# Stick-breaking weights from differenced values, and a re-ordered opening, in a fused encoder block

## The chip, the cores and the metric

One core of a Trainium2 chip runs the whole kernel as one program. The metric is device time in microseconds (us) of that core; lower is better. Engines are TensorE (PE, its weight loads PEld), VectorE (DVE), ScalarE (ACT), GpSimd (POOL) and SyncE (SP, which only issues transfers). The core has 16 DMA engines, which all queues share.

## The reference, cut to what matters

One layer over 512 tokens and 1024 channels, float32. The opening is an adaLN-modulated RMS norm and the input projection:

```python
mod = c_act @ mod_w[l] + mod_b[l]
sh1, sc1, g1, sh2, sc2, g2 = [m[:, None, :] for m in jnp.split(mod, 6, axis=-1)]
h = rms_norm(x, norm1_g[l]) * (1.0 + sc1) + sh1
proj = h @ w_in[l]
```

The columns of `proj` go to a convolution branch, an HGRN2 recurrence and stick-breaking attention (8 heads of 64), whose core, per block of 128 queries, is

```python
z = jnp.einsum('bhtd,bhsd->bhts', qb, kb).astype(jnp.float32) * scale
mask = s_pos[None, :] < t_pos[:, None]
log_keep = jnp.where(mask, jax.nn.log_sigmoid(-z), 0.0)
between = lax.cumsum(log_keep, axis=3, reverse=True) - log_keep
a = jnp.where(mask, jnp.exp(jax.nn.log_sigmoid(z) + between), 0.0)
outs.append(jnp.einsum('bhts,bhsd->bhtd', a.astype(vb.dtype), vb))
```

The three branches are gated, summed and projected; a squared-ReLU MLP follows.

## The kernel before, in words

The kernel is one Python function that records instructions; a scheduler then fixes the order in each engine's queue. From there on each engine takes its queue strictly in order, and an instruction that waits holds up all behind it. Products are float32 split in a rounded part and a rest (`hilo`, L83 on ACT and L84 on DVE), so each product is three matmuls (`mm3`, L113 to L115).

**Opening.** For each of eight blocks j of 128 input channels it needs a scale and a shift column from `mod_w`. `prep_mod(j)` multiplies eight 128x256 pieces of the loaded tile `ms` by `cact` and adds them up (two on ACT, L236, six on DVE, L238), adds the two partial sums (L241) and sums over the partitions with two matmuls against ones (`tp`, L245). `prep_h(j)` transposes the normed x (`tq`, L254), scales and shifts it into `s` (ACT, L258) and splits it into `ht`. `prep_w(j)` splits the 384 KB slab of `w_in`. `first_mm(j)` then issues 18 matmuls into six accumulators (`mm` and `f`). The loads `ms` (two halves of 512 KB for each j, three buffers) and `slab` stand in SP's queue behind the four tiles of x; the small `vecs` and `conv_w` (31 rows of 2 KB) go on ACT's queue.

**Attention.** `sv_in` copies the value rows out of PSUM (L521). For each pair of heads `sb_split` splits queries and keys (ACT L507 to L510, DVE L508 and L511), and `sb_weights` makes scores `z` (PE, L539 to L541), takes sigmoid(-z) and sigmoid(z) (ACT, L88, tile `bt`), scans the first into running products (DVE, L545) and multiplies the second by it (DVE, L546); `sb_turn` transposes the weights (PE, L557), ACT copies them back (L560), and PE multiplies them with the values (L573). Gate products `g` of `head_gate` and the convolution's taps (`cv`, DVE, L462) are recorded beside it and fill gaps.

The scheduler's order is the order of work; `tc.issue_after(x)` keeps instructions behind instruction x on x's engine.

Of the kernel before, what the change touches and what calls it, by code (L numbers as in the profile page):

```python
# [13 lines left out]
ALU = mybir.AluOpType  # L14
# [24 lines left out]
def tile_hybrid_block(ctx, tc, x, vecs, mod_w, mod_b, w_in, conv_w, w_conv, w_hgrn, w_sb, w_out, w1, w2, out):  # L39
# [42 lines left out]
    def hilo(src, hi, lo):  # L82
        A.activation(hi, src, AF.Copy)  # L83
        V.tensor_tensor(out=lo, in0=src, in1=hi.bitcast(F32), op=ALU.subtract)  # L84

    def after(bi, *args, **kw):
        with tc.issue_after(bi.ins):
# [22 lines left out]
    def mm3(o, lhs, rhs, start, stop):  # L110
        lh, ll = lhs
        rh, rl = rhs
        TE.matmul(o, lhsT=lh, rhs=rh, start=start, stop=False)  # L113
        TE.matmul(o, lhsT=lh, rhs=rl, start=False, stop=False)  # L114
        TE.matmul(o, lhsT=ll, rhs=rh, start=False, stop=stop)  # L115


    vrow = S((NVEC, P), g="c0")
    A.dma_start(vrow, vecs)
    cw_row = S((CW, 512), g="c0")  # L120
    A.dma_start(cw_row, conv_w)
# [40 lines left out]
    eps = C([P, 1], F32)  # L162
    G.memset(eps, EPS)
    scanm = C([P, NT, P], F32)
    G.memset(scanm, 1.0)
    G.memset(scanm[:, :, 0:1], 0.0)
# [6 lines left out]
    cp = ax()  # L173
    for i in range(4):
        TE.transpose(cp[:, i * 32:i * 32 + CW], cw_row[:, i * P:(i + 1) * P], ident[0:CW, 0:CW])
    cwc = C([P, 4, 32], F32)
    V.tensor_copy(cwc[:, :, 0:CW], cp[:, 0:128].rearrange("p (i k) -> p i k", k=32)[:, :, 0:CW])
# [9 lines left out]
    oml = C([P, 4], F32)  # L187
    lb = vcol[:, V_HLB:V_HLB + 4]
    lbe = C([P, 4], F32)
    lbs = C([P, 4], F32)  # L190
    V.tensor_tensor(out=lbe, in0=lb, in1=lb, op=ALU.subtract)
    ph(lbe, lbe, AF.Exp)
    V.reciprocal(out=lbs, in_=lbe)
    V.tensor_tensor(out=lbe, in0=lbe, in1=lbs, op=ALU.mult)
    V.tensor_tensor(out=lbs, in0=lbe, in1=lbe, op=ALU.subtract)
    V.tensor_scalar(out=oml, in0=lbs, scalar1=-1.0, scalar2=1.0, op0=ALU.mult, op1=ALU.add)

    gbh = C([P, 24], F32)
    V.tensor_scalar(out=gbh, in0=vcol[:, V_GB:V_GB + 24], scalar1=0.5, scalar2=None, op0=ALU.mult)
    lnh = C([P, 8], F32)  # L200
    V.tensor_scalar(out=lnh, in0=vcol[:, V_LG:V_LG + 8], scalar1=0.5, scalar2=None, op0=ALU.mult)
# [7 lines left out]
    modc = C([P, 16], F32)  # L209


    facc = [mm() if i < 4 else ps("f") for i in range(6)]
    hT, fw = [], {}


    def rstd_small(dst, ssq, n):
# [5 lines left out]
    def x_norm(t):  # L222
        junk = P4((P, D), g="x0")
        after(first, junk, xt[t], AF.Square, accum_out=stat[:, t:t + 1])
        rstd_small(stat[:, 4 + t:5 + t], stat[:, t:t + 1], D)
        V.tensor_scalar(out=xt[t], in0=xt[t], scalar1=stat[:, 4 + t:5 + t], scalar2=None, op0=ALU.mult)

    def prep_mod(j):
        ms = ms_t.pop(j)
        acc = S((P, 2, 2, P), g="acc")  # L230
        for kk in range(KT):
            a, src, c = acc[:, kk % 2], ms[:, :, kk, :], cact[:, kk:kk + 1]
            if kk < 2 and j == 0:
                V.tensor_scalar(out=a, in0=src, scalar1=c, scalar2=None, op0=ALU.mult)
            elif kk < 2:
# [27 lines left out]

    def prep_w(j):
# [4 lines left out]
    def prep(j):  # L269
        load_ms(j)  # L270
        load_slab(j)
        prep_mod(j)
        prep_h(j)
        prep_w(j)

    def first_mm(j):
        wh, wl = fw.pop(j)
        for i in range(6):
            c = slice(i * P, (i + 1) * P)
            mm3(facc[i], (wh[:, c], wl[:, c]), hT[j], j == 0, j == KT - 1)  # L280


    wu = ps("tq")
    for i in range(8):
        TE.matmul(wu, lhsT=ident, rhs=scanm.rearrange("p a t -> p (a t)"), start=True, stop=True)
    for t in range(NT):
        x_norm(t)
    prep_mod(0)
    prep_h(0)
    prep_w(0)  # L290
# [209 lines left out]
    def sb_split(i):  # L500
# [22 lines left out]

    so2 = [P4(g="so") for _ in range(2)]
# [271 lines left out]
    hnh = C([P, 1], F32)  # L796
    V.tensor_scalar(out=hnh, in0=vcol[:, V_HN:V_HN + 1], scalar1=0.5, scalar2=None, op0=ALU.mult)

    for h in range(4):
        k_in(h)  # L800
# [277 lines left out]
```

## Time and profile before

| | |
|---|---|
| median of 3 runs | 922.27 us (921.96 to 922.89) |
| the profiled execution, its own time | 924.09 us |
| its span, first to last instruction | 922.3 us |
| busy PE | 894.8 us (97%) |
| busy DVE | 599.5 us (65%) |
| busy ACT | 385.8 us (42%) |
| mean granted TensorE clock | 0.996 |

Busy time is the union of an engine's instructions. What counts for the time is where PE has none: 27.5 us of the span. The profiled execution is 1.8 us above the median; its span equals the median to 0.1 us.

### The profile page before, as it was taken

How to read it: one execution, taken by the hardware profiler on the slowest of the kernel's cores; microseconds unless marked ns; L12 is line 12 of the kernel's file. 1: busy time of each engine (PE TensorE's matmuls, PEld its weight loads, DVE VectorE, ACT ScalarE, POOL GpSimd, SP SyncE). 2: the span in 40 equal slices, each digit the busy share in tenths (PEclk: the TensorE clock that was granted, in tenths of full speed). 3: DMA queues.
4: the chain of work that ended last, by engine and by line, in shares of the span. 5: the costliest groups of instructions: out<-in, count | busy, mean ns of one | idle time of the engine just before them, and what ended most of it. 6: DMA issues, size and time to landing. Idle time of an engine off the chain costs nothing.

```text
span 922.3 us, 10624 instructions
## 1 busy us (share of the span) xinstructions
PE 894.8 (97%) x4185; PEld 728.8 (79%) x4185; DVE 599.5 (65%) x886; ACT 385.8 (42%) x596; POOL 28.1 (3%) x35
## 2 busy tenths in 40 slices
PE   4999989999988999999999999999999999999998
PEld 2788878888755588888888888888888888888886
DVE  4882388899999999997965544774423254442422
ACT  4652434475788632223833536453312123431210
POOL 1002000001032000000000000000000000000000
PEclk9999999999999999999999999999999999999999
DMA  9981301131200344793423620552242233142121
GB/s 279 279 268 59 113 12 46 52 132 46 91 1 1 115 159 162 245 329 136 138 86 103 216 70 1 192 196 91 92 137 92 56 113 106 46 137 92 68 69 46
DMA packets 85418, 107.78 MB, mean 117 GB/s; under 512 B 2270, under 2 KB 58705, under 8 KB 85368
## 3 DMA queue, kind: packets, MB, share of 16 engines
q1 hardware_dynamic: 85200, 106.96, 35.5%
q8 instruction: 33, 0.54, 0.3%
q14 instruction: 17, 0.14, 0.1%
q10 hardware_dynamic: 168, 0.14, 0.0%
HBM read 105.00 MB, written 2.10 MB: 116 GB/s over the span
## 4 chain that ended last, share of the span: by engine, by line
PE 88%; DVE 6%; ACT 3%; DMA 2%; issue 1%; SPq 1%; DVEq 0%; ACTq 0%
PE mm L113 14%; PE mm L114 14%; PE mm L115 14%; PE ax L115 9%; PE ax L113 9%; PE ax L114 9%; PE o L115 2%; PE o L114 2%; PE o L113 2%; PE g L113 2%; PE g L114 2%; PE g L115 2%; PE g L654 1%; DVE bt L545 1%; PE o L573 1%; DVE bt L546 1%
## 5 line engine op out<-in xcount | busy, mean ns | idle before, releaser
L84 DVE TENSOR_TENSOR wl<-w,wh 128x1024 fp32r<-128x1024 f32 x134 | 162.8, 1221 | 194.4 <-ACT wh L83 147.4
L83 ACT ACTIVATE wh<-w 128x1024 fp32r<-128x1024 f32 x134 | 139.8, 1054 | 290.8 <-PE ax L115 129.9
L113 PE MATMUL mm<-ht,wh 128*128 128x512 f32 x272 | 106.7, 392 | 0.0
L115 PE MATMUL mm<-ht,wl 128*128 128x512 f32 x272 | 106.6, 392 | 0.0
L114 PE MATMUL mm<-ht,wh 128*128 128x512 f32 x272 | 106.6, 392 | 0.0
L114 PE MATMUL mm<-p,wh 128*128 128x512 f32 (+1 forms) x272 | 102.6, 378 | 0.0
L115 PE MATMUL mm<-p,wl 128*128 128x512 f32 (+1 forms) x272 | 102.4, 377 | 0.0
L113 PE MATMUL mm<-p,wh 128*128 128x512 f32 (+1 forms) x272 | 102.3, 377 | 0.0
L462 DVE SCALAR_TENSOR_TENSOR cv<-cv,cbig 128x511 f32<-128x511 f32 (+29 forms) x120 | 83.5, 733 | 0.0
L113 PEld LDWEIGHTS mm<-ht,wh 128*128 128x128 f32 x272 | 51.1, 188 | 11.2 <-issue 0.8
L114 PEld LDWEIGHTS mm<-ht,wh 128*128 128x128 f32 x272 | 51.1, 188 | 11.0 <-issue 0.6
L115 PEld LDWEIGHTS mm<-ht,wl 128*128 128x128 f32 x272 | 51.1, 188 | 10.4 <-issue 0.2
L114 PEld LDWEIGHTS mm<-p,wh 128*128 128x128 f32 x272 | 51.2, 188 | 9.4
L115 PEld LDWEIGHTS mm<-p,wl 128*128 128x128 f32 x272 | 51.2, 188 | 9.4
L113 PEld LDWEIGHTS mm<-p,wh 128*128 128x128 f32 x272 | 51.0, 188 | 9.3
L113 PE MATMUL ax<-wh,p 128*128 128x512 f32 x128 | 49.8, 389 | 0.0
L114 PE MATMUL ax<-wl,p 128*128 128x512 f32 x128 | 49.8, 389 | 0.0
L115 PE MATMUL ax<-wh,p 128*128 128x512 f32 x128 | 49.8, 389 | 0.0
L113 PE MATMUL ax<-wh,s 128*128 128x512 f32 x128 | 49.8, 389 | 0.0
L114 PE MATMUL ax<-wl,s 128*128 128x512 f32 x128 | 49.8, 389 | 0.0
L115 PE MATMUL ax<-wh,s 128*128 128x512 f32 x128 | 49.8, 389 | 0.0
L865 DVE SCALAR_TENSOR_TENSOR s<-p,cbig,s 128x512 f32<-128x512 f32 x64 | 47.1, 746 | 1.5 <-DMA p<-in_mod_w_dram 1.2
(248 smaller groups left out, 1666.8 us busy)
## 6 DMA issues: line engine op xcount, KB each, us to landing
w<-in_w_dram SPq DMA_DIRECT2D x32, 1024.0 KB, 5.7
w<-in_w_in_dram SPq DMA_DIRECT2D x27, 1024.0 KB, 5.3
p<-in_mod_w_dram SPq DMA_DIRECT2D x32, 512.0 KB, 7.4
ms<-in_mod_w_dram SPq DMA_DIRECT2D x16, 512.0 KB, 5.9
w<-in_w_out_dram SPq DMA_DIRECT2D x4, 1024.0 KB
slab<-in_w_in_dram SPq DMA_DIRECT2D x8, 384.0 KB, 4.6
x<-in_x_dram SPq DMA_DIRECT2D x4, 512.0 KB, 8.9
w<-in_w_hgrn_dram SPq DMA_DIRECT2D x2, 1024.0 KB, 4.9
```

Of the source, the lines that this page charges most:

```text
L83: A.activation(hi, src, AF.Copy)
L84: V.tensor_tensor(out=lo, in0=src, in1=hi.bitcast(F32), op=ALU.subtract)
L113: TE.matmul(o, lhsT=lh, rhs=rh, start=start, stop=False)
L114: TE.matmul(o, lhsT=lh, rhs=rl, start=False, stop=False)
L115: TE.matmul(o, lhsT=ll, rhs=rh, start=False, stop=stop)
L462: V.scalar_tensor_tensor(out=cacc[i][:, d:], in0=cu[i][:, 0:T - d], scalar=w, in1=cacc[i][:, d:], op0=ALU.mult, op1=ALU.add)
L545: V.tensor_tensor_scan(out=kp[:, 0:n][:, ::-1], data0=kp[:, 0:n][:, ::-1], data1=kp[:, 0:n][:, ::-1], initial=1.0, op0=ALU.mult, op1=ALU.b ...
L546: V.tensor_tensor(out=bt[:, 0:n - 1], in0=bt[:, 0:n - 1], in1=kp[:, 1:n], op=ALU.mult)
L573: TE.matmul(o[h * 64:h * 64 + 64, sb * P:T], lhsT=svt[sb][:, pr * P + h * 64:pr * P + h * 64 + 64], rhs=ahs[h][bi][:, off:off + n], start= ...
L654: TE.matmul(o[:, b * n:(b + 1) * n], lhsT=l, rhs=r, start=True, stop=True)
L865: V.scalar_tensor_tensor(out=a, in0=box["s"][:, kk, :], scalar=cact[:, 2 * k2 + kk:2 * k2 + kk + 1], in1=a, op0=ALU.mult, op1=ALU.add)
```

## The change

It has two parts. **Values.** The weights are no longer made by a product. With K the running products of sigmoid(-z), the weight of key s is the difference of two neighbouring K, and the sum over s is re-arranged so that K itself (less 1) multiplies differences of neighbouring value rows. The second sigmoid and the 32 products L546 go; the copy back adds -1. The value rows shifted by one partition are made by copies inside the on-chip memory, on ACT's queue: four of 127 rows of 2 KB and three of one row. VectorE then subtracts (L554).

```diff
     def sv_in():
         sv = row_group("sv")
         sv2 = [P4(g="sv") for _ in range(2)]
+        pv2 = [P4(g="pv") for _ in range(2)]
         for t in range(NT):
-            svt.append(sv2[t // 2][:, t % 2, :])
-            A.activation(svt[t], sv[t], AF.Copy)
+            v, pv = sv2[t // 2][:, t % 2, :], pv2[t // 2][:, t % 2, :]
+            svt.append(v)
+            A.activation(v, sv[t], AF.Copy)
+            if t == 0:
+                G.memset(pv[0:1, :], 0.0)
+            else:
+                A.dma_start(pv[0:1, :], svt[t - 1][P - 1:P, :])
+            A.dma_start(pv[1:P, :], v[0:P - 1, :])
+        for t in range(NT):
+            V.tensor_tensor(out=svt[t], in0=pv2[t // 2][:, t % 2, :], in1=svt[t], op=ALU.subtract)
...
-            bt, kp = S(g="bt"), S(g="bt")
+            kp = S(g="bt")
             ph(kp[:, 0:n], z[:, 0:n], AF.Sigmoid, scale=-0.125)
-            ph(bt[:, 0:n], z[:, 0:n], AF.Sigmoid, scale=0.125)
...
-            V.tensor_tensor(out=bt[:, 0:n - 1], in0=bt[:, 0:n - 1], in1=kp[:, 1:n], op=ALU.mult)
-            be.append(bt)
+            be.append(kp)
...
-            A.activation(at[:, 0:n], banks[bi][:, 0:n], AF.Copy)
+            A.activation(at[:, 0:n], banks[bi][:, 0:n], AF.Identity, bias=neg1[:, 0:1])
```

**Opening.** x is loaded on ACT's queue; `conv_w` is loaded later, and its transposes stand later in PE's queue; the sums of block 0 are 16 matmuls on the raw tile instead of work on DVE; for the other blocks the add L241 gives way to two more matmuls; a few small columns are computed elsewhere; `issue_after` pins the preparation of blocks 1 to 7 behind that of block 0 on ACT and DVE, and the sums and transposes of each next block into the middle of the current block's 18 matmuls. Six warm-up matmuls are left of eight. The four `k_in` are pinned behind the middle of the last block.

```diff
+    load_ms(0)
     for t in range(NT):
         xt.append(P4((P, D), g="x0"))
-        SY.dma_start(xt[t], x_v[t])
-    load_ms(0)
+        with tc.issue_after(vdma.ins):
+            A.dma_start(xt[t], x_v[t])
...
+        for q in range(2):
+            if ms is not None:
+                for kk in range(KT):
+                    TE.matmul(tp[:, q:q + 1], lhsT=ms[:, q, kk, :], rhs=cact[:, kk:kk + 1], start=(kk == 0), stop=(kk == KT - 1))
+                continue
+            for e in range(2):
+                TE.matmul(tp[:, q:q + 1], lhsT=acc[:, e, q, :], rhs=ones[:, 0:1], start=(e == 0), stop=(e == 1))
...
+            with tc.issue_after(last[0].ins), tc.issue_after(last[1].ins):
+                acc = prep_mod(j)
+                prep_w(j)
+        mid = first_mm(j - 1, range(3))
+        if j < KT:
+            with tc.issue_after(mid.ins):
+                prep_sum(j, acc)
+                prep_h(j)
+        first_mm(j - 1, range(3, 6))
+        if j == 2:
+            lb_columns()
+        if j == 4:
+            conv_columns()
```

How the queues then stand, at the places that matter. ScalarE's queue in the opening, before (`s` and `ht` belong to one block, `acc<-ms` to a later one):

```order
L258 ACTIVATE s_187<-tq_182,cbig_73 128x512
L236 ACTIVATE acc_253<-ms_248,cbig_73 128x256
L83 ACTIVATE ht_188<-s_187 128x512
L236 ACTIVATE acc_253<-ms_248,cbig_73 128x256
L83 ACTIVATE fwh_278<-slab_251 128x768
L258 ACTIVATE s_221<-tq_216,cbig_73 128x512
L83 ACTIVATE ht_222<-s_221 128x512
```

and in the change (`ms_182`, `ms_235` and `ms_297` are those of blocks 1, 2 and 3):

```order
L271 ACTIVATE s_177<-tq_172,cbig_73 128x512
L83 ACTIVATE ht_178<-s_177 128x512
L244 ACTIVATE acc_187<-ms_182,cbig_73 128x256 x2
L83 ACTIVATE fwh_196<-slab_185 128x768
L244 ACTIVATE acc_240<-ms_235,cbig_73 128x256 x2
L83 ACTIVATE fwh_249<-slab_238 128x768
L83 ACTIVATE fwh_311<-slab_300 128x768
L244 ACTIVATE acc_302<-ms_297,cbig_73 128x256
L271 ACTIVATE s_221<-tq_216,cbig_73 128x512
L244 ACTIVATE acc_302<-ms_297,cbig_73 128x256
L83 ACTIVATE ht_222<-s_221 128x512
```

Before, block 1's `s` (`s_221`) stood behind the modulation of block 2 (`acc_253`); now it stands behind the first half of that of block 3 (`acc_302`), and the second half stands between it and its `ht`. SP's queue in the change, from its start:

```order
L137 DMA slab_87<-in_w_in_dram 128x768
L128 DMA ms_76<-in_mod_w_dram 128x8x128
L137 DMA slab_185<-in_w_in_dram 128x768
L128 DMA ms_182<-in_mod_w_dram 128x8x128
L128 DMA ms_76<-in_mod_w_dram 128x8x128
L137 DMA slab_238<-in_w_in_dram 128x768
L128 DMA ms_182<-in_mod_w_dram 128x8x128
L128 DMA ms_235<-in_mod_w_dram 128x8x128 x2
L137 DMA slab_300<-in_w_in_dram 128x768
L137 DMA slab_353<-in_w_in_dram 128x768
L137 DMA slab_414<-in_w_in_dram 128x768
L137 DMA slab_467<-in_w_in_dram 128x768
L128 DMA ms_297<-in_mod_w_dram 128x8x128 x2
```

Four slabs, of blocks 3 to 6, now stand ahead of block 3's `ms`; before, slab and `ms` came by turns. VectorE's queue at the start of the attention, before (the splits of the first pair, between taps):

```order
L462 SCALAR_TENSOR_TENSOR cv_615<-cv_608,cbig_73,cv_615 128x491
L508 TENSOR_TENSOR p4_1919<-qr_1475,p4_1919 64x512
L511 TENSOR_TENSOR kl_1921<-qr_1649,p4_1920 64x512
L84 TENSOR_TENSOR wl_2242<-w32_2062,wh_2241 128x1024
L462 SCALAR_TENSOR_TENSOR cv_615<-cv_608,cbig_73,cv_615 128x491
L508 TENSOR_TENSOR p4_1919<-qr_1475,p4_1919 64x512
```

and in the change (L554 are the four subtractions, L530 and L533 are the former L508 and L511; `p4_1924` and `p4_1925` hold the shifted rows):

```order
L554 TENSOR_TENSOR p4_1922<-p4_1924,p4_1922 128x512
L484 SCALAR_TENSOR_TENSOR cv_625<-cv_618,cbig_73,cv_625 128x488
L84 TENSOR_TENSOR wl_2371<-w32_2368,wh_2370 128x1024
L554 TENSOR_TENSOR p4_1923<-p4_1925,p4_1923 128x512
L530 TENSOR_TENSOR p4_1942<-qr_1484,p4_1942 64x512
L554 TENSOR_TENSOR p4_1923<-p4_1925,p4_1923 128x512
L533 TENSOR_TENSOR kl_1944<-qr_1658,p4_1943 64x512
L530 TENSOR_TENSOR p4_1942<-qr_1484,p4_1942 64x512
L533 TENSOR_TENSOR kl_1944<-qr_1658,p4_1943 64x512
```

The splits that the first scores need now stand behind the third and the fourth subtraction. On PE, 42 matmuls of two `g` tiles stand between the last value product and the first score; before there were 11. Its queue there in the change:

```order
L114 MATMUL g_2220<-ht_451,wh_1894 128x512
L115 MATMUL g_2220<-ht_451,wl_1895 128x512
L572 MATMUL z_1957<-p4_1943,p4_1942 128x256
L572 MATMUL z_1964<-p4_1943,p4_1942 128x256
L113 MATMUL g_2220<-ht_504,wh_1894 128x512
L114 MATMUL g_2220<-ht_504,wh_1894 128x512
L115 MATMUL g_2220<-ht_504,wl_1895 128x512
L113 MATMUL g_2220<-ht_557,wh_1894 128x512
L573 MATMUL z_1957<-kl_1944,p4_1942 128x256
```

Four more `g` matmuls stand between the first two score matmuls and the third, which reads `kl`.

## Rows read from the trace of the kernel before

**Rows 1.** Busy time by stretch: length, PE, PEld, DVE, ACT, POOL, clock, DMA share, GB/s.

```profile
0.00:10.00 10.00, 0.42 (x1) 0.18 (x1) 0.28 (x1) 2.53 (x4) 3.70 (x17) 1.00 0.82 281
10.00:20.00 10.00, 9.09 (x22) 4.36 (x23) 6.54 (x26) 6.19 (x19) 0.00 (x0) 1.00 0.94 260
20.00:30.00 10.00, 6.91 (x35) 5.55 (x34) 7.62 (x20) 4.72 (x8) 0.00 (x0) 0.83 1.15 319
240.00:280.00 40.00, 36.24 (x180) 25.66 (x178) 39.47 (x62) 34.47 (x71) 8.15 (x4) 1.00 0.12 42
280.00:300.00 20.00, 18.28 (x96) 12.54 (x97) 19.46 (x31) 16.94 (x39) 4.23 (x4) 1.00 0.01 1
300.00:320.00 20.00, 18.81 (x98) 11.24 (x96) 19.94 (x35) 12.17 (x28) 0.99 (x2) 1.00 0.24 76
```

**Rows 2.** Timeline of PE, opening: start, length, instruction, count, idle before and its releaser.

```profile
10.91 0.63 PE L175 MATMUL ax<-crs,c 31*128 31x31 f32 x4 [5.71 <-DMA c<-in_conv_w_dram]
19.88 0.95 PE L245 MATMUL tp<-crs,acc 128*128 128x1 f32 x8
25.06 2.07 PE L113 MATMUL mm<-ht,fwh 128*128 128x512 f32 x4 [2.63 <-ACT ht L83]
```

**Rows 3.** Chain that ended last, opening: start, length, what.

```profile
31.30 0.44 PE tq L254 x4
31.73 0.24 PE mm L113
61.84 0.92 PE mm L113 x4
```

**Rows 4.** Timeline of ACT, opening.

```profile
1.33 0.24 ACTq L121 DMA_DIRECT2D c<-in_conv_w_dram  x1
22.71 0.78 ACT L258 ACTIVATE s<-tq,cbig 128x512 f32<-128x512 f32 x1 [2.04 <-DVE cbig L248]
23.98 0.51 ACT L236 ACTIVATE acc<-ms,cbig 128x256 f32<-128x256 f32 x1 [0.49 <-DMA ms<-in_mod_w_dram]
24.40 0.61 ACT L83 ACTIVATE ht<-s 128x512 fp32r<-128x512 f32 x1
39.46 1.28 ACT L100 ACT_TABLE_LOAD   x1
```

**Rows 5.** DMA issues of the whole run: count, KB each, median us to landing.

```profile
ms<-in_mod_w_dram SPq DMA_DIRECT2D x16, 512.0 KB, 5.9
slab<-in_w_in_dram SPq DMA_DIRECT2D x8, 384.0 KB, 4.6
```

**Rows 6.** DMA queue of ACT, 0 to 4.25 us, then 4.25 to 11 us: packets, MB, share.

```profile
q10 hardware_dynamic: 120, 0.06, 4.8%
...
q10 hardware_dynamic: 32, 0.06, 2.5%
```

**Rows 7.** DMA, 900 to 923 us: SP's queue, and the output's issues.

```profile
q1 hardware_dynamic: 576, 1.05, 12.1%
...
out_dram<-p SPq DMA_DIRECT2D x4, 256.0 KB, 2.0
```

**Rows 8.** Timelines of ACT, SP, PE and DVE at the attention's start.

```profile
244.72 1.09 ACT L521 ACTIVATE p<-ax 128x512 f32<-128x512 f32 x2
...
249.08 0.37 SPq L329 DMA_DIRECT2D w<-in_w_in_dram  x1
...
245.95 0.39 PE L115 MATMUL ax<-wh,ht 128*128 128x512 f32 x1
246.18 0.39 PE L113 MATMUL g<-ht,wh 128*128 128x512 f32 x1
...
248.96 0.38 PE L539 MATMUL z<-p,p 128*128 128x256 f32 x1
...
247.23 0.68 DVE L511 TENSOR_TENSOR kl<-qr,p 64x512 fp32r<-64x512 f32 x1
```

**Rows 9.** Groups of the whole run: count, busy us, mean ns, idle before and releaser.

```profile
L546 DVE TENSOR_TENSOR bt<-bt 128x127 f32<-128x127 f32 (+3 forms) x32 | 15.6, 510 | 0.2
```

More of the change, by code (lines that the diff above doesn't have):

```diff
@@ L82, in hilo @@
     def hilo(src, hi, lo):
-        A.activation(hi, src, AF.Copy)
-        V.tensor_tensor(out=lo, in0=src, in1=hi.bitcast(F32), op=ALU.subtract)
+        a = A.activation(hi, src, AF.Copy)
+        return a, V.tensor_tensor(out=lo, in0=src, in1=hi.bitcast(F32), op=ALU.subtract)
     def after(bi, *args, **kw):
@@ L114, in mm3 @@
         TE.matmul(o, lhsT=lh, rhs=rl, start=False, stop=False)
-        TE.matmul(o, lhsT=ll, rhs=rh, start=False, stop=stop)
+        return TE.matmul(o, lhsT=ll, rhs=rh, start=False, stop=stop)
     vrow = S((NVEC, P), g="c0")
-    A.dma_start(vrow, vecs)
-    cw_row = S((CW, 512), g="c0")
-    A.dma_start(cw_row, conv_w)
+    vdma = A.dma_start(vrow, vecs)
     x_v = x.rearrange("(a p) d -> a p d", p=P)
@@ L161, in tile_hybrid_block @@
     ones, ident = onesr.bitcast(F32), identr.bitcast(F32)
-    eps = C([P, 1], F32)
+    eps, neg1 = C([P, 1], F32), C([P, 1], F32)
     G.memset(eps, EPS)
+    G.memset(neg1, -1.0)
     scanm = C([P, NT, P], F32)
@@ L172, in tile_hybrid_block @@
     V.tensor_copy(vcol, vp[:, 0:NVEC])
[L173 to L177, printed above, removed]
     cact = C([P, 8], F32)
@@ L184, in tile_hybrid_block @@
     V.tensor_tensor(out=cact, in0=vcol[:, V_C:V_C + 8], in1=ctmp, op=ALU.mult)
[L187 to L201, printed above, removed]
     mb_v = mod_b.rearrange("(o m) -> o m", o=1)
@@ L209, in tile_hybrid_block, with conv_columns, lb_columns @@
     modc = C([P, 16], F32)
+    cwc = C([P, 4, 32], F32)
+    oml = C([P, 4], F32)
+    gbh = C([P, 24], F32)
+    lnh = C([P, 8], F32)
+    hnh = C([P, 1], F32)
+    def conv_columns():
+        cw_row = S((CW, 512), g="c0")
+        with tc.issue_after(hb[3].ins):
+            A.dma_start(cw_row, conv_w)
+        cp = ax()
+        for i in range(4):
+            TE.transpose(cp[:, i * 32:i * 32 + CW], cw_row[:, i * P:(i + 1) * P], ident[0:CW, 0:CW])
+        V.tensor_copy(cwc[:, :, 0:CW], cp[:, 0:128].rearrange("p (i k) -> p i k", k=32)[:, :, 0:CW])
+    def lb_columns():
+        lb = vcol[:, V_HLB:V_HLB + 4]
+        lbe = C([P, 4], F32)
+        lbs = C([P, 4], F32)
+        V.tensor_tensor(out=lbe, in0=lb, in1=lb, op=ALU.subtract)
+        ph(lbe, lbe, AF.Exp)
+        V.reciprocal(out=lbs, in_=lbe)
+        V.tensor_tensor(out=lbe, in0=lbe, in1=lbs, op=ALU.mult)
+        V.tensor_tensor(out=lbs, in0=lbe, in1=lbe, op=ALU.subtract)
+        V.tensor_scalar(out=oml, in0=lbs, scalar1=-1.0, scalar2=1.0, op0=ALU.mult, op1=ALU.add)
+        V.tensor_scalar(out=gbh, in0=vcol[:, V_GB:V_GB + 24], scalar1=0.5, scalar2=None, op0=ALU.mult)
+        V.tensor_scalar(out=lnh, in0=vcol[:, V_LG:V_LG + 8], scalar1=0.5, scalar2=None, op0=ALU.mult)
+        V.tensor_scalar(out=hnh, in0=vcol[:, V_HN:V_HN + 1], scalar1=0.5, scalar2=None, op0=ALU.mult)
     facc = [mm() if i < 4 else ps("f") for i in range(6)]
-    hT, fw = [], {}
+    hT, fw, hb = [], {}, []
     def rstd_small(dst, ssq, n):
@@ L225, in x_norm @@
         rstd_small(stat[:, 4 + t:5 + t], stat[:, t:t + 1], D)
-        V.tensor_scalar(out=xt[t], in0=xt[t], scalar1=stat[:, 4 + t:5 + t], scalar2=None, op0=ALU.mult)
+        b = V.tensor_scalar(out=xt[t], in0=xt[t], scalar1=stat[:, 4 + t:5 + t], scalar2=None, op0=ALU.mult)
+        return ph.ops[-1], b
     def prep_mod(j):
@@ L232, in prep_mod @@
             a, src, c = acc[:, kk % 2], ms[:, :, kk, :], cact[:, kk:kk + 1]
-            if kk < 2 and j == 0:
-                V.tensor_scalar(out=a, in0=src, scalar1=c, scalar2=None, op0=ALU.mult)
-            elif kk < 2:
+            if kk < 2:
                 A.activation(a, src, AF.Identity, scale=c)
@@ L238, in prep_mod, with prep_sum @@
                 V.scalar_tensor_tensor(out=a, in0=src, scalar=c, in1=a, op0=ALU.mult, op1=ALU.add)
-        ne = 2 if j == 0 else 1
-        if ne == 1:
-            V.tensor_tensor(out=acc[:, 0], in0=acc[:, 0], in1=acc[:, 1], op=ALU.add)
+        return acc
+    def prep_sum(j, acc=None):
         tp = ps("tp")
+        ms = None if acc is not None else ms_t.pop(j)
         for q in range(2):
-            for e in range(ne):
-                TE.matmul(tp[:, q:q + 1], lhsT=acc[:, e, q, :], rhs=ones[:, 0:1], start=(e == 0), stop=(e == ne - 1))
+            if ms is not None:
[4 more added lines that the diff above has]
+                TE.matmul(tp[:, q:q + 1], lhsT=acc[:, e, q, :], rhs=ones[:, 0:1], start=(e == 0), stop=(e == 1))
         gs, sh = modc[:, j:j + 1], modc[:, 8 + j:9 + j]
@@ L258, in prep_h @@
         b = A.activation(hf, tq, AF.Identity, scale=gs, bias=sh)
+        hb.append(b)
         if j == 3:
             ph.ops.append(b)
-        hilo(hf, hh, hl)
         hT.append((hh, hl))
+        return hilo(hf, hh, hl)
     def prep_w(j):
@@ L267, in prep_w, with first_mm @@
         fw[j] = (wh, wl)
[L269 to L278, printed above, removed]
+    def first_mm(j, tiles):
+        wh, wl = fw[j]
+        for i in tiles:
             c = slice(i * P, (i + 1) * P)
-            mm3(facc[i], (wh[:, c], wl[:, c]), hT[j], j == 0, j == KT - 1)
+            b = mm3(facc[i], (wh[:, c], wl[:, c]), hT[j], j == 0, j == KT - 1)
+        return b
     wu = ps("tq")
-    for i in range(8):
+    for i in range(6):
         TE.matmul(wu, lhsT=ident, rhs=scanm.rearrange("p a t -> p (a t)"), start=True, stop=True)
+    prep_sum(0)
     for t in range(NT):
[L287 to L290, printed above, removed]
+        last = x_norm(t)
+    with tc.issue_after(last[0].ins), tc.issue_after(last[1].ins):
+        prep_w(0)
+    last = prep_h(0)
     for j in range(1, KT + 1):
         if j < KT:
-            prep(j)
-        first_mm(j - 1)
+            load_ms(j)
+            load_slab(j)
+            with tc.issue_after(last[0].ins), tc.issue_after(last[1].ins):
+                acc = prep_mod(j)
[10 more added lines that the diff above has]
+            conv_columns()
     dij = S((P, P), I32, g="mk")
@@ L794, in conv_norm @@
             V.scalar_tensor_tensor(out=cacc[i], in0=th, scalar=1.0, in1=cacc[i], op0=ALU.add, op1=ALU.mult)
[L796 to L800, printed above, removed]
+    with tc.issue_after(mid.ins):
+        for h in range(4):
+            k_in(h)
     HP[0] = 2000
```

## Prediction

> **What bounds the kernel now.** I read the busy time by stretch first. PE is without work for 27.5 us of the 922.3; in the stretches shown that is 13.6 us in the first 30 us and 6.7 us between 240 and 320 us [rows 1]. So the kernel is bound by PE, and mostly those two places can give anything back; whatever makes PE wait elsewhere, or gives it more to do, is added in full. Then the chain of waits through the opening: the first product starts at 25.06 us, behind `ht` [rows 2]; from block 1 (31.73 us) to block 7 (61.84 us less 0.2) the products follow each other without a stop, 4.99 us for each block [rows 3]. Third the timelines of the attention's start: the last value product starts at 245.95 us, the first score at 248.96 us, and what lies between is `g` work [rows 8]. There VectorE is the one that is full: 39.47 of 40 us, 19.46 of 20 and 19.94 of 20 [rows 1].
>
> **The values.** Removed: 32 products on VectorE, 15.6 us [rows 9], and 32 of 64 sigmoids on ScalarE. Added: four subtractions of some 0.68 us, the time of the two-input operation on half the partitions and as many columns [rows 8], 2.7 us. VectorE so gains 12.9 us where it is full and PE has its 6.7 us of gaps. I take it that 4.7 us of the gaps go and 2 us stay (waits for transposes and weight loads that no VectorE work ends): **-4.7 us**, bounds 0 and -6.7.
>
> Now the copies. The four subtractions wait for four copies of 127 rows of 2 KB, and VectorE's splits for the first score stand behind the third and fourth of them; VectorE is in order, so taps, weight splits and scans wait there too. What does such a copy take? No copy inside the memory stands in the trace, so I bound it. The nearest row by shape is `conv_w`, 31 rows of 2 KB. From 4.25 us on its queue moved 32 packets [rows 6]: 31 rows and one completion. The output's copies of 128 rows left 576 packets for 512 rows [rows 7], that is 16 completions for each. So 128 rows are dealt to 16 engines, and 31 rows went through one. `vecs` with its 115 rows made the other 120 packets, five completions. 115 can be shared evenly by five engines, 31 by none, and neither can 127. So I put 127 rows on one engine; the other bound is sixteen. One packet of 2 KB takes 2.5% of 16 engines over 6.75 us, 2.70 us, by 31: 0.087 us; the output's, read from on-chip memory, take 12.1% of 16 x 23 us by 512: also 0.087 us [rows 6, 7]. A copy is then 127 x 0.087 = 11.0 us on one engine, 0.7 us on sixteen.
>
> Do the four lie on the same engine? `conv_w` was issued at 1.33 us [rows 4], and none of its packets moved before 4.25 us, though `vecs` held only five engines [rows 6]. It queued behind `vecs`; engines are not picked because they are free. I take one engine for all four, one after another: 508 packets, 44.2 us. The bound below is four engines side by side.
>
> The Trainium skill, page "DMA: Bandwidth & Descriptors", section "Why a DMA increments its semaphore by 16 and not by 1", has a rule that speaks against this change: such a transfer is shared by the largest number of engines, up to 16, that divides its slowest dimension, 127 partitions go to one, and it is always the lowest-numbered ones. By that rule the four copies queue on one engine and the sum is the one below; if it failed for 127 rows, the sum would be the 926 us of a rival below. The trace agrees as far as 31 and 115 rows go (one and five completions); 127 rows are in no run here.
>
> On the path: the second value copy out of PSUM ends at 245.3 us (244.72 + half of the pair) [rows 8], and the first shifted copy is issued behind it. Fixed time of issue and landing: the output's 256 KB take 2.0 us to land, of which 8 packets are 0.7 [rows 7]: 1.3 us. Packets: 44.2 us. A load of 1 MB is issued at 249.08 us [rows 8]; its sixteenth, 32 times 2 KB by the same price, shares the engine: 2.8 us. The last rows so land at 293.6; the subtraction (0.68) and the split of the keys (0.68) [rows 8] bring PE to 295.0 us. PE's cover is the `g` work: 42 matmuls from 246.18 at 0.2275 us (245.95 to 246.18 is one [rows 8]), to 255.7 us, and four more later, 0.9 us, which I leave out. PE stops for **39.3 us**. After a stop the clock falls: after the 2.63 us of idling before the first product [rows 2] the stretch was granted 0.83 of full speed, 1.7 us of 10 [rows 1]; I add **+1.5 us**. Sum of the part: 39.3 + 1.5 - 4.7 = **+36.1 us**. ScalarE's issue of seven copies and its waits lie beside this stop.
>
> **The opening.** x on ACT's queue no longer stands before `ms` and the slabs. Up to the second half of block 0's `ms` the queues hold x (512 x 1024 values, 2.10 MB), two slabs (0.79) and three halves (1.57), 4.46 MB [rows 5]; at the first stretches' 281 and 260 GB/s [rows 1] that lands at 16.3 us. Eight of the 16 sums are left then, two instructions each at 0.12 us (0.95 us for eight [rows 2]), 1.9 us; then columns 0.2, `s` 0.78, `ht` 0.61 [rows 4]: first product at about 20 us, 5 us earlier. Its 18 matmuls, sums and transposes end by 27 us. But block 1's `s` now stands behind the first half of block 3's modulation on ScalarE, which needs block 3's `ms`; ahead of that are seven slabs, eight halves and x, 9.04 MB [rows 5]. Before had moved 8.60 MB at 30 us [rows 1]; I take 30.5 us. Modulation, `s`, modulation, `ht`: 0.4 + 0.78 + 0.4 + 0.61, the next product at 32.7 us, where before had 31.73: **+1.0**. The 5 us are lost.
>
> From there each block costs PE 18 x 0.2275 = 4.10, the sums eight instructions instead of four, 0.95 [rows 2], and the transposes 0.44 [rows 3]: 5.49 against 4.99, six times: **+3.0**. Half clock after the stop of 27 to 32.7: **+1.5**. The sums and transposes of the next block stand in the middle, with eight matmuls (1.8 us) behind them; columns, `s` and `ht` need 1.7, and with a modulation of 0.4 between `s` and `ht` 2.1, 0.3 too much, four times: **+1.2**. The table load of 1.28 us stands there once [rows 4]: **+0.7** over what it cost before. `conv_w` took 9.6 us from its issue to its transposes (1.33 to 10.91) [rows 2, 4]; it is now issued in block 3 and its transposes stand one block (5.4 us) later on PE: **+1.5**, between 0 and 4. Sum **+8.9 us**, bounds -2.0 (the 5 us kept, the extra sums paid) and +13 (`ms` 2 us later, `conv_w` at its upper end). The add L241, the small columns, the two warm-up matmuls and pinned `k_in` cost or give nothing: they lie in VectorE's slack or before the loads have landed; without that cover they would be under 1 us each.
>
> **Sum.** 922.3 + 36.1 + 8.9 = **967.3, taken as 967 us**. That is against the span, which equals the median of the runs to 0.1 us; the profiled execution itself would be 969 us.
>
> **The rivals.**
> - *Four engines.* Each copy is alone on an engine of its own, all side by side. The last is issued at 248.3 us and ends 1.3 + 11.0 later; PE starts at 262, 6.3 us after its cover. 922.3 + 8.9 + 6.3 + 1.5 - 4.7 = 934 us. For it: nothing; against it, that `conv_w` waited for `vecs`. 0.06.
> - *Sixteen engines.* The copies take 0.7 us each and land under the cover; the opening stays as it is: 922.3 + 8.9 - 4.7 = 926 us. For it: the output's 128 rows; against it, the single completion of 31. 0.06.
> - *The other side, faster.* Transfers cost their bytes alone, at more than before shows, because two queues now feed the engines: at 0.39 MB/us block 3's `ms` lands at 25 us and PE goes from block 0 to block 1 without a stop (opening +8.9 - 5.3 - 1.5 = +2.1), and the copies land in 2 us. 922.3 + 2.1 - 4.7 = 920 us. It decides where block 3's `ms` lands by 27 us and a copy has at least five engines (44.2 us by five is 8.8, under the cover of 9.6). For it: the 319 GB/s of 20 to 30 us [rows 1]; against it the same 31 rows. 0.05.
> - *Slower packets.* If packets from on-chip to on-chip memory take 0.12 us, the stop is 17 us longer: 984 us. It is in the range of the forecast, since both prices there are are 0.087.
>
> **How the numbers follow.** The forecast, one engine for all, has 0.83; its own range is 952 (opening at -2.0, no shared load, all 6.7 us of gaps gone) to 983 (opening at +13, packets of 0.11). To leave out no more than 2 in 10 the range takes in the four engines: **933 to 988 us**. A measurement of this kernel can tell about 0.2% (1.8 us) from no change. Faster by more than that: 0.04, most of the rival on the other side. Within: 0.02. Slower: 0.94.
>
> **What would show it.** In the profile after: the four subtractions start some 11 to 12 us apart, with VectorE waiting for a DMA before each; PE has one gap of 35 to 45 us in front of the attention's first scores, and nearly none in the rest of that stage; ACT's queue has 4 x 128 packets more on one engine. In the opening the first product is at 20 us, the second block's at 32 to 33, the last accumulator some 8 us later than before. The prediction is wrong if the subtractions follow each other within 3 us, or if block 1's products start before 29 us.

## The result and the profile after

The changed kernel takes 970.63 us (median, 969.33 to 971.7) against 922.48 of the kernel before: ratio 1.0522, 95% interval 1.0503 to 1.0540, 48.1 us slower. The forecast was 967 with a range of 933 to 988. The traced execution has a span of 968.5 us, where the sum of the prediction gave 967.3.

Two lines of the page of the profile after: busy time by engine, and ScalarE's DMA queue (packets, MB, share).

```profile
PE 908.6 (94%) x4233; PEld 740.5 (76%) x4233; DVE 586.7 (61%) x843; ACT 380.1 (39%) x564; POOL 27.9 (3%) x37
...
q10 hardware_dynamic: 1352, 3.28, 0.9%
```

PE is busy 13.8 us longer than before (908.6 against 894.8) and without work 32.4 us longer (59.9 against 27.5). So nearly a third of the loss is no waiting at all. Where the loss lies shows in the busy time by stretch of the kernel after (columns as in [rows 1]):

```profile
30.00:40.00 10.00, 7.80 (x25) 6.64 (x26) 4.37 (x11) 6.07 (x9) 0.00 (x0) 0.55 1.06 278
...
260.00:270.00 10.00, 6.33 (x28) 4.89 (x27) 2.12 (x3) 0.61 (x2) 0.00 (x0) 1.00 0.38 123
270.00:280.00 10.00, 0.00 (x0) 0.00 (x0) 2.35 (x4) 0.60 (x1) 0.00 (x0) 0.50 0.07 26
280.00:290.00 10.00, 0.00 (x0) 0.00 (x0) 2.47 (x3) 5.08 (x8) 0.00 (x0) 0.50 0.07 26
290.00:300.00 10.00, 2.47 (x6) 1.59 (x6) 1.38 (x2) 0.00 (x0) 0.00 (x0) 0.50 0.07 25
300.00:310.00 10.00, 7.43 (x31) 6.54 (x32) 8.30 (x12) 5.76 (x11) 0.00 (x0) 0.63 0.01 3
310.00:320.00 10.00, 8.64 (x46) 5.55 (x45) 9.83 (x15) 8.59 (x18) 3.15 (x2) 1.00 0.00 0
320.00:340.00 20.00, 18.17 (x96) 11.05 (x94) 18.92 (x27) 14.60 (x29) 8.56 (x6) 0.91 0.01 2
340.00:360.00 20.00, 18.68 (x101) 12.14 (x100) 18.86 (x29) 13.37 (x26) 0.00 (x0) 1.00 0.17 53
```

From 270 to 290 us PE does nothing and VectorE and ScalarE little, and DMA is busy for 0.07 of 16 engines: about one DMA engine, at 26 GB/s. What is waited for shows in VectorE's timeline of the kernel after (L554 are the four subtractions):

```profile
269.10 0.69 DVE L554 TENSOR_TENSOR p<-p,p 128x512 f32<-128x512 f32 x1 [7.72 <-DMA p<-p]
280.91 0.69 DVE L554 TENSOR_TENSOR p<-p,p 128x512 f32<-128x512 f32 x1 [8.56 <-DMA p<-p]
291.15 0.69 DVE L554 TENSOR_TENSOR p<-p,p 128x512 f32<-128x512 f32 x1 [7.77 <-DMA p<-p]
301.14 0.69 DVE L554 TENSOR_TENSOR p<-p,p 128x512 f32<-128x512 f32 x1 [8.58 <-DMA p<-p]
```

Each waits for its copy, 11.8, 10.2 and 10.0 us after the one ahead. PE's timeline of the kernel after, first the first products of blocks 0, 1, 2 and 6, then the first and third score, answers to [rows 2, 3, 8]:

```profile
21.03 2.07 PE L113 MATMUL mm<-ht,fwh 128*128 128x512 f32 x4 [1.58 <-ACT ht L83]
32.20 2.07 PE L113 MATMUL mm<-ht,fwh 128*128 128x512 f32 x4 [3.99 <-ACT ht L83]
41.92 1.09 PE L113 MATMUL mm<-ht,fwh 128*128 128x512 f32 x4
67.66 1.20 PE L113 MATMUL mm<-ht,fwh 128*128 128x512 f32 x4 [0.54 <-ACT ht L83]
...
292.71 0.77 PE L572 MATMUL z<-p,p 128*128 128x256 f32 x2 [26.38 <-DVE p L530]
302.57 0.55 PE L573 MATMUL z<-kl,p 128*128 128x256 f32 x1 [7.39 <-DVE kl L533]
```

The stop is two gaps, 26.38 and 7.39 us, 33.8 together, with two score and four `g` matmuls between them. The opening: block 1's products start at 32.20 us (31.49 before, in the same view), but block 1 then takes 9.72 us, without a gap, four of its matmuls 2.07 us where block 2's take 1.09. That is the clock of 0.55 in 30 to 40 us.

### The profile page after: what moved, and what is told of

Same layout as the page of the kernel before. It is cut to its first block, busy times and chain, and to the rows that moved or that the text cites. A ratio compares the mean times of both kernels' runs of the same rounds, so it can differ in the third digit from the quotient of the medians.

```text
span 968.5 us, 10619 instructions
## 1 busy us (share of the span) xinstructions
PE 908.6 (94%) x4233; PEld 740.5 (76%) x4233; DVE 586.7 (61%) x843; ACT 380.1 (39%) x564; POOL 27.9 (3%) x37
## 4 chain that ended last, share of the span: by engine, by line
PE 84%; DVE 6%; DMA 4%; issue 2%; ACT 2%; SPq 2%; ACTq 1%
PE mm L113 13%; PE mm L114 13%; PE mm L115 13%; PE ax L113 8%; PE ax L115 8%; PE ax L114 8%; PE o L113 2%; PE o L114 2%; PE o L115 2%; DMA p<-p 2%; PE g L114 2%; PE g L115 2%; PE g L113 2%; DVE bt L577 2%; PE g L685 1%
## 5 line engine op out<-in xcount | busy, mean ns | idle before, releaser
L83 ACT ACTIVATE wh<-w 128x1024 fp32r<-128x1024 f32 x134 | 140.5, 1056 | 309.2 <-PE ax L115 136.1
L894 DVE SCALAR_TENSOR_TENSOR s<-p,cbig,s 128x512 f32<-128x512 f32 x64 | 47.2, 746 | 1.5 <-DMA p<-in_mod_w_dram 1.2
```

The costliest lines, as they stand in the source:

```text
L83: a = A.activation(hi, src, AF.Copy)
L894: V.scalar_tensor_tensor(out=a, in0=box["s"][:, kk, :], scalar=cact[:, 2 * k2 + kk:2 * k2 + kk + 1], in1=a, op0=ALU.mult, op1=ALU.add)
```

## Experiments

The kernel before was timed again beside each set: 920.87 us in the first, 922.35 in the second, 922.11 in the third, 922.02 in the last. Times of different sets are compared by their ratios to it. The kernels of the first set take the change apart.

**Even copies.** 127 rows are cut into counts that many DMA engines can share:

```diff
-            A.dma_start(pv[1:P, :], v[0:P - 1, :])
+            for r0, r1 in ((0, 112), (112, 127)):
+                A.dma_start(pv[1 + r0:1 + r1, :], v[r0:r1, :])
```

> The changed kernel with each shifted copy of 127 rows cut into one of 112 and one of 15 rows, all else as it is. Theory (a row count that no number of engines shares evenly goes through one engine, and the four copies queue there): 112 rows are 7 packets on each of 16 engines and 15 rows one packet on each of 15, so a copy takes under 2.5 us, the four subtractions follow each other within 4 us in all, PE has no gap over 3 us before the first scores, and what is left of the 48 us is the opening's 10.5 (last value product at 256.42 us against 245.95) less 0 to 6.7 of the gaps of before: 926 to 933 us. Rival (copies from on-chip to on-chip memory are slow by themselves, or what is slow is the issue on ScalarE's queue, which now holds twice as many copies): subtractions still 8 us or more apart, 960 us or more.

Measured: 933.42 us, ratio 1.0130 (1.0106 to 1.0154). By the ratios 36 us of the 48 are gone, by the row counts alone; PE is 9.84 of 10 us busy between 265 and 275. The subtractions were further apart than expected (262.4 to 272.4 us), but none waits for a DMA. The packets of ScalarE's queue tell how many DMA engines took part, since each engine adds a completion to the rows: first the kernel with the opening alone, which has no copies, then this one.

```profile
q10 hardware_dynamic: 744, 2.24, 0.6%
```

```profile
q10 hardware_dynamic: 1472, 3.28, 1.0%
```

The kernel after has 608 more than the first of these, which is 4 x (127 + 1) and 3 x 32 for the one-row copies, themselves cut in 16. Here 728 more: 4 x (112 + 16 + 15 + 15) and 3 x 32. So 127 rows went to one engine, 112 to sixteen and 15 to fifteen.

**Values alone, opening alone.** The diff's hunks of one part are put on the kernel before: for the values `sv_in`, `sb_weights` and the copy back of `sb_turn`; for the opening all the others.

> The kernel before with the values part of the change alone (copies of 127 rows, subtractions, one sigmoid, no products); the opening is that of before. Theory (the two parts add up): 922.5 + 48.1 - 10.5 = 960 us, between 955 and 965, with the same four waits of VectorE, 8 to 12 us each. Rival (the parts hide each other: the late opening pushes the stop to a worse place, or the queue of copies is fed late because ScalarE is late from the opening): under 950 us.

> The changed kernel with the values part taken back (products of two sigmoids, no copies, no subtractions); the opening is that of the change. Theory (the opening costs what the last value product shows, 10.5 us, and nothing gives it back since PE has no slack behind it): 933 us, between 930 and 936. Rival (VectorE, which starts the attention later, finds PE's gaps of 240 to 320 us already filled): 925 to 928 us.

Measured: values 957.13 us, ratio 1.0382 (1.0359 to 1.0404); opening 934.37 us, ratio 1.0134 (1.0114 to 1.0155). That is 36.3 and 13.5 us, and the two ratios multiply to 1.0521, for 1.0522 of both: the parts add up. By the traces the opening's part is smaller, 933.0 against 922.3, 10.7 us; the traced execution of the kernel before is 1.6 us above its median (924.09 for 922.48). Busy time by engine, on the pages of the kernel with the values alone and then of the one with the opening alone:

```profile
PE 899.7 (94%) x4185; PEld 733.0 (77%) x4185; DVE 590.5 (62%) x858; ACT 379.6 (40%) x564; POOL 27.9 (3%) x37
```

```profile
PE 904.5 (97%) x4233; PEld 736.9 (79%) x4233; DVE 595.6 (64%) x871; ACT 387.2 (42%) x596; POOL 28.2 (3%) x36
```

With the values alone PE has the 4185 instructions of before and is busy 4.9 us longer (894.8). That is taken as half clock: after the stop the clock is 0.60 in 290 to 300 us and 0.91 in 320 to 340. With the opening alone it is busy 9.7 us longer and idle only 1.0 us longer (933.0 - 904.5 = 28.5). This is a balance: the first product comes 4 us sooner, and block 1 then waits 4 us. The opening has 52 column sums more and four warm-up instructions fewer. At 0.119 us (0.95 by eight [rows 2]) the 48 are an estimated 5.7 us, of which 24 sums stand ahead of the first product; block 1 at half clock is another 4.2 us (9.72 us for 5.49).

**Even copies on the opening of before.** The same cut, with the values part alone.

> The kernel before with the values part alone and its copies cut into 112 and 15 rows. Theory (without the queue on one engine the part is the saving it looks like: 32 products of VectorE and 32 sigmoids of ScalarE go, and VectorE was full between 240 and 320 us): 916 to 922 us, some 2 to 5 us of PE's gaps in front of and among the first scores gone. Rival (PE's gaps there have another cause than VectorE, or the copies, subtractions and key splits behind them cost what is gained): 922 to 926 us.

Measured: 921.88 us, ratio 1.0002 (0.9991 to 1.0014). The theory fell, although the time is at the edge of its range: 32 products and 32 sigmoids went, and by the ratio nothing came of it. 240 to 320 us of the kernel before and of this one, and the taps there (columns of [rows 1] and [rows 9]):

```profile
240.00:320.00 80.00, 73.33 (x372) 49.45 (x370) 78.86 (x126) 63.58 (x135) 13.37 (x10) 1.00 0.12 40
...
L462 DVE SCALAR_TENSOR_TENSOR cv<-cv,cbig 128x494 f32<-128x494 f32 (+11 forms) x23 | 16.1, 727 | 0.0
```

```profile
240.00:320.00 80.00, 73.95 (x375) 50.81 (x374) 79.14 (x115) 56.42 (x105) 12.66 (x9) 1.00 0.22 73
...
L463 DVE SCALAR_TENSOR_TENSOR cv<-cv,cbig 128x493 f32<-128x493 f32 (+18 forms) x37 | 25.5, 731 | 0.1
```

VectorE is as full as it was (79.14 of 80 us). 15.6 us of products left, 2.7 us of subtractions came, and 14 more taps, 9.4 us, were drawn ahead into the room. PE's gaps went from 6.7 to 6.1 us.

**Two engines.** In the changed kernel the copies are cut at 122 rows:

```diff
-            A.dma_start(pv[1:P, :], v[0:P - 1, :])
+            for r0, r1 in ((0, 122), (122, 127)):
+                A.dma_start(pv[1 + r0:1 + r1, :], v[r0:r1, :])
```

> The changed kernel with each shifted copy of 127 rows cut into 122 and 5 rows. 122 is twice 61, and 61 is prime, so two engines take 61 packets each and five take one more. Theory (the stop is packets on one engine, 10.0 us for 127 between two subtractions, 0.079 us each): 62 packets a copy on the fuller engine, subtractions 4.9 us apart, the last one 20 us earlier than at 301.1 us, and the stop is shorter by as much: 970.6 - 20.5 = 950 us, between 946 and 953. Rival (a fixed time for every copy, whatever its rows): nine copies more or less as long as before, 965 us or more.

Measured: 940.86 us, ratio 1.0199 (1.0169 to 1.0230). VectorE's timeline of this kernel, the subtractions:

```profile
263.21 0.69 DVE L555 TENSOR_TENSOR p<-p,p 128x512 f32<-128x512 f32 x1 [1.70 <-DMA p<-p]
268.20 0.69 DVE L555 TENSOR_TENSOR p<-p,p 128x512 f32<-128x512 f32 x1 [0.61 <-DMA p<-p]
273.24 0.69 DVE L555 TENSOR_TENSOR p<-p,p 128x512 f32<-128x512 f32 x1 [2.43 <-DMA p<-p]
277.95 0.69 DVE L555 TENSOR_TENSOR p<-p,p 128x512 f32<-128x512 f32 x1 [1.42 <-DMA p<-p]
```

They are 4.7 to 5.0 us apart, half of 10.0, which fits 62 packets of 0.079 us in place of 127. The queue has 24 packets more than that of the kernel after, 4 x (122 + 2 + 5 + 5 - 128): two engines for 122 rows and five for 5. The time fell by 30 us where 20.5 were expected. The last subtraction is 23.2 us earlier, the first copy being shorter too; and the order put more `g` work ahead of the first score, so that PE's cover ends at 271.2 us and not at 266.3. PE's stop is 5.3 us, for 33.8.

**Two queues.** In the changed kernel the last two of the four copies go by another queue:

```diff
-            A.dma_start(pv[1:P, :], v[0:P - 1, :])
+            (A if t < 2 else SY).dma_start(pv[1:P, :], v[0:P - 1, :])
```

> The changed kernel with the third and fourth copy of 127 rows issued on SyncE's queue in place of ScalarE's. Theory (the engine is given by the row count and is the same one for every queue, so that the copies share it): the last subtraction starts within 3 us of 301 us and the time stays at 966 to 973 us, although ScalarE no longer stands in its issue for so long. Rival (each queue deals to engines of its own, or the stop is ScalarE's queue that is full): the two pairs run side by side, the last subtraction starts at some 281 us, 949 to 953 us.

Measured: 967.83 us, ratio 1.0493 (1.0473 to 1.0513); the last subtraction starts at 299.67 us. The subtractions are 19.3, 2.6 and 8.8 us apart, so the copies of the two queues held each other up: the queues share one DMA engine, and a free ScalarE is worth at most 3 us. The Trainium skill, page "DMA: Bandwidth & Descriptors", section "Why a DMA increments its semaphore by 16 and not by 1", gives the rule: 127 rows go to one engine, always the lowest-numbered. The packets agree with the counts for 5, 15, 112, 122 and 127 rows, and this run with one engine for both queues; which number the engine has no run here shows.

**Pinned taps.** On the kernel before with the values part and even copies, the taps from the 37th on stand behind the last scan of the attention:

```diff
-    taps = list(bg)
+    def late(f):
+        with tc.issue_after(scan[0].ins):
+            f()
+
+    taps = [f if n < 36 else (lambda f=f: late(f)) for n, f in enumerate(bg)]
```

> The kernel before with the values part and copies of 112 and 15 rows (measured at 921.9 us beside 920.9 of before), and besides that all convolution taps from the 37th on issued behind the last scan of the attention. Theory (the 13 us that the values part frees on VectorE were filled with 14 taps that the order draws ahead, 37 taps in 240 to 320 us for 23 before, so that the scans PE waits for came no sooner): without taps between the scans PE's 6.1 us of gaps there fall to 1 to 2, and the time is 916 to 918 us. Rival (PE's gaps there come from the order of transposes, copies and products itself, or the late taps hold up the convolution's sums): 921 us or more.

Measured: 919.51 us, ratio 0.9969 (0.9953 to 0.9985), faster than before by about 0.3%, though less than the theory wanted: PE's gaps fell to 4.3 us, not to 1 or 2. The control has the same pin on the kernel before, with its products:

> The kernel before with the convolution taps from the 37th on issued behind the last scan of the attention, and nothing else (both sigmoids and the 32 products stay). Theory (what PE waits for between 240 and 320 us is VectorE's whole load there, whatever it consists of): taking the 23 taps of that stretch away, 16 us, does as much as the values part and the pinned taps did together (ratio 0.997), 918 to 920 us. Rival (the products are on the way from a scan to its transposes, so that they cost PE by themselves): 921 us or more.

Measured: 922.76 us, ratio 1.0011 (1.0002 to 1.0021): no gain. 240 to 320 us of the kernel with even copies and pinned taps, then of the control with PE's wait for the products:

```profile
240.00:320.00 80.00, 75.75 (x386) 52.71 (x385) 62.44 (x88) 58.02 (x109) 12.33 (x9) 1.00 0.23 73
```

```profile
240.00:320.00 80.00, 73.61 (x375) 50.21 (x375) 72.19 (x115) 64.38 (x138) 17.55 (x8) 1.00 0.14 44
...
PE tb L559 <- DVE bt L548: 5.5, 8, 1.4
```

The control frees VectorE by 6.7 us (78.86 to 72.19), and PE's gaps stay at 6.4 us: for 5.5 of them it waits for the products on the way to the transposes (L548). Without the products but with taps, they stay at 6.1 too. Only without the products and with fewer taps (9 in this stretch, for 23 before and 12 in the control) do they fall, to 4.3. That the load and the way from scan to transposes each hold PE by themselves is one reading. The other, that VectorE's load alone counts and 72.19 us are still too many where 62.44 are not, is not excluded by these runs.

**Opening in the order of the blocks.** On the changed kernel with even copies, each load stands behind the one before it, `w` loads behind the last of them, and blocks 3 to 7 are prepared behind `prep_h(j - 2)`:

```diff
-            SY.dma_start(ms_t[j][:, q], mw_v[:, :, c0:c0 + P])
+            load(ms_t[j][:, q], mw_v[:, :, c0:c0 + P])
...
-    last = prep_h(0)
+    done = [prep_h(0)]
...
+            last = done[max(j - 2, 0)]
             with tc.issue_after(last[0].ins), tc.issue_after(last[1].ins):
                 acc = prep_mod(j)
```

> The changed kernel with copies of 112 and 15 rows (measured at 933.4 us) and an opening in which the loads are issued in the order of the blocks and the modulation and weight split of block j stand behind block j-2's transposed activations on ScalarE and VectorE, so that block 1's no longer wait for block 3's loads. Theory (that wait, from 27.8 to 32.2 us on PE, and the half clock behind it are most of the opening's cost): block 1's products start at 28 to 29 us, block 7's at 61.5 to 64 instead of 73.4, and the time is 921 to 925 us. Rival (the extra instructions and the late table load and convolution weights are most of it, 5.5 us a block and more): block 7 at 68 us or later, 928 us or more.

Measured: 925.87 us, ratio 1.0047 (1.0029 to 1.0066), by the ratios 7.7 us less than with even copies alone and just outside the expected range. Block 1's products start at 24.98 us, but block 7's not before 66.92. PE's timeline of this kernel shows why:

```profile
46.05 0.40 PE L207 MATMUL ax<-crs,c 31*128 31x31 f32 x4 [3.43 <-DMA c<-in_conv_w_dram]
```

The transposes of the convolution's weights, which the early blocks now reach sooner, wait 3.43 us for their load, and from 47.9 to 54.6 us the granted clock is 0.50. So they were issued at `j == 6` in place of `j == 4`:

> The kernel with copies of 112 and 15 rows and the opening in the order of the blocks (measured at 925.9 us), and the convolution weights' transposes issued two blocks later on PE, their load where it was. Theory (PE stood still for 3.4 us for that load and then ran 6.7 us at half clock, which cost 3.1 more): 919.4 us, between 918 and 921, block 7's products at 60 to 61 us instead of 66.92. Rival (the clock or the next wait, the loads of the last blocks, takes the place): 923 us or more.

Measured: 922.81 us, ratio 1.0005 (0.9995 to 1.0014). Block 7's products come at 61.41 us, near the 60 to 61 expected, but the time falls by the ratios by 3.9 us, of the 6.5 expected; by the traces it is 4.1 (925.8 to 921.7). With the pinned taps besides:

> As the kernel before this one in the list, and with the taps from the 37th on issued behind the last scan. Theory (the opening and the attention's stretch are apart in time, so that the two gains add: 919.4 and the ratio of 0.997): 916 to 918 us, faster than the kernel before by some 0.5%. Rival (the taps, later by as much as VectorE no longer needs, hold up the convolution now that everything else is earlier): 919 us or more.

Measured: 920.01 us, ratio 0.9982 (0.9968 to 0.9997). The gain of the pins comes on top, but less of it than expected (0.0023 of the ratio for 0.0031), and the kernel is no better than the opening of before with the same values part (0.9969): in the kernel without the pins, whose first product comes at 17.48 us, block 7 starts at 61.41 us, and before it started at 61.68. The lead of 7.6 us is spent on the way: block 0 takes 9.07 us (26.55 - 17.48) for 6.43 before, and each of the next six 5.81 for 5.03. One more tries to take the four added sums per block back:

```diff
+        V.tensor_tensor(out=acc[:, 0], in0=acc[:, 0], in1=acc[:, 1], op=ALU.add)
         return acc
...
-            for e in range(2):
-                TE.matmul(tp[:, q:q + 1], lhsT=acc[:, e, q, :], rhs=ones[:, 0:1], start=(e == 0), stop=(e == 1))
+            TE.matmul(tp[:, q:q + 1], lhsT=acc[:, 0, q, :], rhs=ones[:, 0:1], start=True, stop=True)
```

> The kernel with copies of 112 and 15 rows, the opening in the order of the blocks, the late convolution weights and the pinned taps (measured at 920.0 us), and with the two halves of each block's modulation added on VectorE again (as before the change), so that PE makes four instructions of column sums for a block in place of eight. Theory (the four more, 0.95 us for eight, are on PE's path in seven blocks and eat most of the opening's earlier start): 7 x 0.475 = 3.3 us less, 916.7 us, between 915.5 and 918. Rival (VectorE's additions of 0.42 us stand before the columns, and PE waits for them): 919 us or more.

Measured: 921.81 us, ratio 0.9996 (0.9986 to 1.0005): no gain. PE's waits on `ht` in the first 70 us, in the kernel with all and in this one:

```profile
PE mm L113 <- ACT ht L83: 2.8, 3, 1.6
```

```profile
PE mm L113 <- ACT ht L83: 4.3, 5, 1.6
```

PE's waits on `ht` grew by 1.5 us. Its busy time fell by 3.7 us (900.4 to 896.7) and the traced span by 2.6, but not the median: the traced execution of this kernel is one of its shortest (919.71 us), that of the other one of its longer ones (922.15). So the gain in the spans is not shown to be one.

## Why the prediction was right, and where its terms were off

**The rule and the place held.** One DMA engine for all four copies had a chance of 0.83. The packets show it, half the packets on two engines bring half the distance, a second queue brings next to nothing, and an even cut takes 36 of 48 us away. The rivals of four and of sixteen engines, at 934 and 926 us, are out; so is that of transfers that cost bytes alone. Sixteen engines did come true by an edit, at 933.42 and not at 926, since the gaps stayed and the opening cost more.

**The stop: 39.3 us forecast, 33.8 measured.** PE's cover ended where it was put: the last `g` matmul before the stop ends at 266.33 us, which less the 10.47 us that the opening shifts everything (last value product at 256.42 for 245.95) is 255.9, for 255.7. The third score was put at 295.0 and came at 302.57 - 10.47 = 292.1. The first copy was issued 1.6 us sooner than taken (254.13 - 10.47 = 243.7 for 245.3): it stands behind the first value copy out of PSUM, and the prediction took the second. The three distances between the subtractions were 32.0 us together, not 33.1, since a packet took 0.079 us, not 0.087, with nothing else on the engine (10.0 us by 127). The rest of the difference is the 2.5 us of scores and `g` that PE did between the two gaps.

**The gaps regained: -4.7 forecast, -2.2 measured** (4.5 us are left from 310 to 360 us, of 6.7). The step that failed took 12.9 us less work on VectorE for 12.9 us of room there. With even copies on the opening of before, 0.6 us of the gaps went: the order fills the room with taps. Where taps were kept out but the products stayed, the gaps stayed too; whether by the way or by the load that was left is open. The bound of 0 had covered this.

**Half clock: 1.5 forecast for this stop, 4.9 measured** with the values alone (3.5 by the busy time of the kernel after against that with even copies, 908.6 - 905.1; 5.9 by the values alone against the same with even copies, 899.7 - 893.8); **1.5 for the opening's stop, about 4.2 measured** (block 1 takes 9.72 us for the 5.49 of the forecast). This term was mis-sized in both places. It was read from 20 to 30 us of before, where a wait of 2.63 us left 0.83; in the kernel after, a wait of 3.99 us left 0.55 in the following stretch, and the long stop left 0.63 in 300 to 310 us though PE was at work.

**The opening: +8.9 forecast, 10.7 measured** by the traces (0.0134 by the ratio, 12.4 us). First product at 21.03 for 20, block 1 at 32.20 for 32.7. The cause was named rightly: block 1's `s` waits behind block 3's modulation. ScalarE's timeline of the kernel after, which answers to [rows 4]:

```profile
30.06 0.51 ACT L244 ACTIVATE acc<-ms,cbig 128x256 f32<-128x256 f32 x1 [5.19 <-DMA ms<-in_mod_w_dram]
30.47 0.76 ACT L271 ACTIVATE s<-tq,cbig 128x512 f32<-128x512 f32 x1
```

The extra sums, +3.0, had the right size: without them, in the last experiment, PE is busy 3.7 us less, though the time did not fall. `conv_w` was put at 1.5 and cost PE a wait of 0.51 us in the kernel after, but 3.43 where the blocks came sooner.

**Sum.** By the measured terms 33.8 - 2.2 + 4.9 + 10.7 = 47.2, for 46.2 between the traces (968.5 - 922.3); the forecast had 45.0. So the total came as close as it did partly by luck, because errors cancel: a stop 5.5 us too long against 2.5 too much regained, 3.4 too little for its half clock and 1.8 too little for the opening. In the signs that were named: "one gap of 35 to 45 us" and "nearly none in the rest of that stage" were wrong, the distances of 11 to 12 us were right for the first and 1 to 2 us too long for the others, and the last accumulator's last matmul came 11.6 us later (77.36 for 65.79), not some 8.

## What to carry to other kernels

Look at the row count of each copy before its bytes: 127 rows of 2 KB took 10 us, and as 112 and 15 rows the same bytes were hidden. When work is taken off a full engine, look at what the order puts in its place; here the products and some of the taps had to go together, for 0.3%. A stop of PE costs its length and the half clock behind it; read that price from a stretch after a stop of the same length.

## What was not expected of the hardware

**Issue that stands still.** ScalarE's timeline of the kernel after, its issues (L551 the one-row copies, L552 those of 127 rows), and behind them a copy out of PSUM (L547) and a weight split (L83):

```profile
254.13 0.72 ACTq L552 DMA_DIRECT2D p<-p  x1
254.89 4.13 ACTq L551 DMA_DIRECT2D p<-p  x1
...
259.80 11.97 ACTq L551 DMA_DIRECT2D p<-p  x1
271.81 0.60 ACT L547 ACTIVATE p<-ax 128x512 f32<-128x512 f32 x1 [11.20 <-issue]
...
272.49 7.91 ACTq L551 DMA_DIRECT2D p<-p  x1
280.50 1.06 ACT L83 ACTIVATE wh<-w 128x1024 fp32r<-128x1024 f32 x1 [8.09 <-issue]
```

Issuing a copy of one row took 4.1 to 12.0 us, and apart from one copy out of PSUM near the start of each of the first two, ScalarE began nothing else meanwhile; with even copies the same three issues took 0.56 to 0.57 us. With two copies on SyncE's queue its second issue took 19.95 us. So in these runs copies that crowd one DMA engine also stopped the engine that issued the next one. That a queue holds only so much for one DMA engine is inferred, not shown.

**The price of a row.** From on-chip to on-chip memory 2 KB took 0.079 us by one DMA engine, 26 GB/s, with hardly anything else on it. The subtraction of the first of the four copies, beside which a load of 1 MB was issued at 261.41 us, started 15.0 us after the copy's issue; those of the last two followed at 10.2 and 10.0. That the load shared the engine fits, but was not tested by itself.
